# A one-layer decoder trunk on one core: new issue orders in the opening and in the experts' loop, and one more expert half in plain fp32

## The chip, the cores and the metric

The kernel runs on one core of one Trainium2 chip. The metric is the device time of one execution in microseconds (us). The time before is the median of three runs; a fourth execution was profiled, and every row of the trace is from that one.

## The reference

One layer with 512 rows of 1024 channels, batch 1, everything in fp32:

- `mod = silu(c) @ w_mod + b_mod` gives three vectors for each of the two halves (shift, scale, gate).
- `h = rms_norm(x) * (1 + sc1) + sh1`; `proj = h @ w_in` feeds three branches (a gated MLP over chunks, gated linear attention, sparse attention with a top-k of keys); `x = x + gt1 * (merged @ w_out)`.
- `h2 = rms_norm(x) * (1 + sc2) + sh2`, then a hierarchical mixture of experts: each row picks one of 4 groups, and in it 2 of 4 experts. For an expert with weights gate, up (1024 x 256 each) and down (256 x 1024):

```python
hg = h2 @ w_exp_gate[e]
hu = h2 @ w_exp_up[e]
y += (silu(hg) * hu * combine[:, e]) @ w_exp_down[e]
```

- `x = x + gt2 * y`.

## The kernel before

**Two kinds of product.** A product of fp32 matrices is mostly made of three products in a reduced type (fp32r). Each operand is split into a high and a low part by `split` (lines 226 and 227): ACT rounds the high part (`...h`), DVE subtracts it from the operand to get the low part (`...l`). `mm3` (line 217) then issues three matmuls, high by high, low by high and high by low. The other kind is the plain fp32 matmul (line 1574 for an expert's gate and up), which needs no split and reads the loaded weights as they are; the trace has two records for one such product of 512 columns.

**The opening** (0 to 59 us) computes the first six column tiles of `h @ w_in`. Its work is cut into some 400 steps, and the string `START` (lines 41 to 57) lists them in the order in which they are issued; a loop reads it and calls a small function for each. The steps that matter here: `wmN` issues N matmuls on a constant tile whose result nobody reads (line 396), so that TensorE is busy; `xeN` copies a finished bank of transposed rows to `xnT`, on ACT (line 319) or, with a V, on DVE (line 321); `whN` and `wlN` split a tile of `w_in` (lines 274, 277); `mp`, `ma`, `mb`, `mj`, `md`, `mo` and `mc` make, for one chunk of 128 channels, the shift and the scale from the loads of `w_mod` (products on ACT, line 331; sums and join on DVE, lines 338 and 342; columns on PE, lines 350 and 358; the final column on DVE, lines 366 and 367); `hh`, `hf` and `hl` make the transposed `h` of that chunk, high, full and low (lines 370, 374, 377); `fIDQ` is one matmul of column tile I with chunk D, Q being the pair of parts (line 387).

**The middle** (59 to about 582 us) holds the three branches and the router. The change does not touch it.

**The experts' loop** (lines 1780 to 1835) makes 17 passes. Passes 0 to 3 are the four experts of the first group, which share one tile of up to 128 rows. Passes 4 to 12 are single experts whose rows are fetched from DRAM by an indirect DMA on POOL (`slots`, line 1491); the pass `EX` = 6 is for rows that overflow the 128 of some expert: it takes its weights by a number known at run time, and pass 7 uses the same weights. Passes from `GL` = 13 are the last group, again on shared rows. Each pass e works on three things: gate and up of expert e (`gate_up`, line 1568, with the eight chunks of 128 channels in four calls of two, then `activate`, line 1578), the transposed activations and the down product of expert e-1 (`act_t`, line 1588; `down`, line 1607), and the weights and rows of expert e+1 (the units of `w_units`, line 1425, which split the weights into `guh`/`gul` and `dnh`/`dnl`; `x_rows`, line 1545, which transposes the rows `X` and splits them into `XTh`/`XTl`, or copies them to `XTf` for a plain half). `native` (line 1418) tells which halves of an expert's gate and up are plain. `overflow` (line 1721) is a generator of small DVE instructions that plan the overflow pass; the loop takes its steps one at a time (`next(ov)`).

**The loads.** 96 loads of 512 KB bring the experts' weights into 24 buffers (`load_raw`, line 1155). The load j+24 is issued when buffer j was last read: by the unit that splits it, or by `used` (line 1461) for a plain half. SP issues them, each behind a hold (line 1177) that reads the tile of an earlier load, so that SP goes on only once that one has landed; before the change this is the load with the number five less.

Of the kernel before, what the change touches and what calls it, by code (L numbers as in the profile page):

```python
# [13 lines left out]
I32 = mybir.dt.int32  # L14
# [22 lines left out]
HOLD_FROM, HOLD_TO, AHEAD = 26, 96, 5  # L37
# [1 line left out]
LV = [1, 2, 4, 8, 16, 32, 64]  # L39

START = """
Lx0 Lx1 Lx2 Lx3 wm9 Lm0 Lu0 Lm1 Lu1 Lm2 Lu2 sq0 sq1 rs0 sc0 sq2 rs1 xt0 sq3 rs2 sc1 sc2 wm3 xt1 rs3 xt2 mp0 sc3 ma0
wm3 xt3 mb0 xs7 xe0A xe2A md0 wh0 mo0 mp1 wl0V Lu3 Lm3 xe1A ma1 xe5A xe3A mc0 wh1 wm6 md1 mb1 hh0 wl1V Lu4 mo1 mp2
f000 md2 mc1 hf0 ma2 f001 hh1 f100 hl0V f101 hf1 mb2 f010 f002 f102 wh3 f011 mj2 f110 f111 hl1V mo2 xe4A f300 wl3V wh2
f302 f012 f112 f310 f312 mc2 mp3 f200 wl2V Lu5 Lm4 Lm5 Lm6 f202 f301 hh2 f210 f212 f311 ma3 hf2 f201 f211 f020 wh4 mb3
Lm7 f021 f120 f121 f220 xe6A f221 f320 f321 xe7A f400 mj3 f402 f410 hl2V mo3 wh5 f412 wl4V f022 f122 f222 f500 mp4 mc3
f502 f401 wl5V f411 hh3 f510 f512 f322 f420 hf3 ma4 f421 f501 f511 f422 mp5 hl3V f520 f521 f522 mb4 f030 f031 f032
f130 f131 f132 f230 mj4 f231 mp6 f232 ma5 mo4 f330 f331 mc4 f332 mb5 f430 hh4 f431 f432 f530 f531 hf4 f532 f040 f041
mp7 mj5 f140 f141 ma6 mo5 f240 mc5 f241 f340 mb6 f341 hh5 f440 f441 f540 f541 hf5 f050 f051 f150 mj6 f151 f250 hl5V
mo6 f251 hl4V f052 f152 mc6 f252 f042 ma7 f142 hh6 f242 f342 f442 mb7 hf6 f542 f350 f351 f352 f450 f451 f452 hl6V f550  # L50
# [122 lines left out]
def trunk(ctx: ExitStack, tc: tile.TileContext, I, out, dbg=None):  # L173
# [7 lines left out]
    V, A, G, T, SY = nc.vector, nc.scalar, nc.gpsimd, nc.tensor, nc.sync  # L181
# [953 lines left out]

    RAWS = ["E"] + ["X"] * 5 + ["MG", "MG", "T1", "T2"]
    NRAW = 2 * len(RAWS) + 4
    raws, ids, duo = {}, {}, {}
    wset = lambda e: e if e <= EX else e - 1

    EX, GL = 6, 13
# [12 lines left out]
    def load_raw(j, hold=False, eng=SY):  # L1154
        if j >= 96:
            return
        e, i = SEQ[j]
        if e >= PRE:
            if e not in ids:
                v = R.ex_i if e == EX else R.perm[:, e - PRE:e - PRE + 1]  # L1160
                ids[e] = nc.sync.value_load(v[0:1], min_val=0, max_val=15)
            e = ids[e]
        if j >= NRAW:
            raws[j] = raws[j - NRAW]
            if j % 2 == 0:
                duo[j] = duo[j - NRAW]
        elif j % 2:
            raws[j] = raws[j - 1, 1]
        else:
            k = RAWS[j // 2] if j < 2 * len(RAWS) else "P"  # L1170
            t = {"X": lambda: R.rawx.tile([128, 2048], FT, name="raw_x"),
                 "P": lambda: R.ep.tile([128, 2048], FT, name="raw_p", bufs=2)}.get(k, lambda: big(k, "raw_e"))()
            raws[j], raws[j, 1] = t[:, 0:1024], t[:, 1024:2048]
            duo[j] = t
        hf = i // 2 if i < 4 else i - 4
        if eng is SY and HOLD_FROM <= j < HOLD_TO:
            SY.value_load(raws[j - AHEAD][0:1, 0:1].bitcast(I32))
        eng.dma_start(raws[j], expert_src(e, i % 2 if i < 4 else 2)[:, hf * 1024:hf * 1024 + 1024])

    def load_x():  # L1180
# [235 lines left out]
    wfull = {}  # L1416

    def native(w):
        return (0, 1) if w < 2 else () if w in (3, EX) or w >= 12 else (1,)

    def native_dn(w):
        return (0, 1) if w == 0 else ()
# [47 lines left out]
    GR0 = range(4)  # L1470
# [46 lines left out]
    def x_group():  # L1517
        X = ep.tile([128, 1024], FT, name="X", bufs=1)
        A.activation(X[:, 0:512], st["X0"][0], AF.Copy)
        V.tensor_copy(X[:, 512:1024], st["X0"][1])  # L1520
        XT_[0], bs = [], []
        for hf in range(2):
            b = bank()
            for k in range(4):
                T.transpose(b[:, k * 128:(k + 1) * 128], X[:, 4 * hf + k::8], ident)
            bs.append(b)
        route()
        for hf in range(2):
            XT = ep.tile([128, 4, 128], FT, name="XTf", bufs=2)
            for k in range(4):  # L1530
                c, g, sh = bs[hf][:, k * 128:(k + 1) * 128], R.mcolx[:, 0, 4 * hf + k:4 * hf + k + 1], R.mcolx[:, 1, 4 * hf + k:4 * hf + k + 1]
                if hf:
                    V.tensor_scalar(XT[:, k], c, g, sh, OP.mult, OP.add)
                else:
                    A.activation(XT[:, k], c, AF.Identity, bias=sh, scale=g)
            XT_[0].append([XT])
        XT_[1] = XT_[0]

    def x_halves(hf):
        XT = [ep.tile([128, 4, 128], FR, name="XT" + x, bufs=2) for x in "hl"]  # L1540
        split(XT[0], XT[1], XT_[0][hf][0])
        for e in GR0[2 + hf:]:
            XT_[e] = [XT, XT_[0][1]] if hf == 0 else [XT_[2][0], XT]

    def x_rows(e):
        if e in GR0:
            return
        if e > GL:
            XT_[e] = XT_[GL]
            return  # L1550
        X = X_.pop(e)
        XT_[e] = []
        for hf in range(2):
            nat = hf in native(wset(e))
            XT = [ep.tile([128, 4, 128], FT, name="XTf", bufs=2)] if nat else [ep.tile([128, 4, 128], FR, name="XT" + x, bufs=2) for x in "hl"]
            b = bank()
            for k in range(4):
                T.transpose(b[:, k * 128:(k + 1) * 128], X[:, 4 * hf + k::8], ident)
            b = b.rearrange("p (k t) -> p k t", k=4)
            if nat:  # L1560
                A.activation(XT[0], b, AF.Copy)
            else:
                split(XT[0], XT[1], b)
            XT_[e].append(XT)
# [3 lines left out]
    def gate_up(e, kts):  # L1568
        if e not in gb:
            gb[e] = bank("mm")  # L1570
        for kt in kts:
            x, w = XT_[e][kt // 4], wfull[wset(e)][0][kt // 2]
            if len(w) == 1:
                T.matmul(gb[e], x[0][:, kt % 4], w[0][:, kt % 2], start=kt == 0, stop=kt == 7)
            else:
                mm3(gb[e], [t[:, kt % 4] for t in x], [t[:, kt % 2] for t in w], kt == 0, kt == 7)
# [200 lines left out]
    ov = overflow()  # L1777
    DN = []
    none = [lambda: None] * 10
    for e in range(NE - 1):  # L1780
        U = none[:4] + U[4:] if e == EX else w_units(wset(e + 1))
        gate_up(e, (0, 1))
        if e in (1, 2):
            x_halves(e - 1)
        for u in U[4:6] if e == EX else U[0:2]:
            u()
        for _ in range((0, 3, 1)[min(e, 2)]):
            next(ov, None)
        gate_up(e, (2, 3))
        used(e, 0)  # L1790
        if e == 0:
            ranks(range(4))
            positions()
            weights()
            one_hot(0)
            hi_lo(R.tw0.rearrange("p t e i -> p e t i"), R.PC[:, 0:4, 5:9])
        else:
            act_t(e - 1)
        for u in U[6:8] if e == EX else U[2:4]:
            u()  # L1800
        x_rows(e + 1)
        if e + 3 <= GL and e > 1:
            slots(e + 3)
        if e + 4 <= GL and e:
            one_hot(e + 4)
# [5 lines left out]
            down(e - 1)  # L1811
        for d in DN[:1]:
            d()
        gate_up(e, (6, 7))
        if e == 0:
            slots(0)
# [12 lines left out]
        for d in DN[1:]:  # L1829
            d()  # L1830
        used(e, 1)
        if e < NE - 2 and e not in (EX - 1, EX):
            U[6]()
            U[7]()
# [90 lines left out]
```

## Time and profile before

| | us |
|---|---|
| median of three runs | 784.78 |
| the three runs | 784.78, 779.66, 784.89 |
| the profiled execution, its own time | 781.99 |
| its span in the trace | 780.3 |
| busy in the span: PE | 744.3 (95%) |
| busy: DVE | 549.1 (70%) |
| busy: ACT | 327.6 (42%) |
| mean granted TensorE clock | 0.989 of full speed |

A timeline row reads: start, time from its start to the end of the last of its xcount instructions, engine, line, operation, output<-inputs, and in brackets how long the engine idled before it and what released it. PE is matmul, DVE VectorE, ACT ScalarE, POOL GpSimd, SPq the queue of SyncE. Matmuls are pipelined, so what one costs is the distance from its start to the next one's, not its duration. In a table by windows the columns are the window, its length, busy time and (count) for PE, weight loads, DVE, ACT and POOL, then the granted clock as a share of full speed, the DMA share and GB/s.

### The profile page before, as it was taken

The numbers are of one execution on the slowest core, as the hardware profiler recorded it, in microseconds if no ns is written. First come the engines' busy times: TensorE is split into PE (matmuls) and PEld (weight loads), VectorE is DVE, ScalarE is ACT, GpSimd is POOL, SyncE is SP. The second block draws the span as 40 slices with busy tenths as digits, with TensorE's granted clock in tenths as the row PEclk, the third lists the DMA queues.
The fourth block names the chain that finished last, engine by engine and source line by source line (L and its number), as shares of the span: only waits on it lengthen the run. The fifth ranks groups of instructions, "written<-read, shape, count | busy, mean of one in ns | idle before, by whom it ended". The sixth has DMA issues, their size and how long they took to land. (4 is left out here: it accounts for less than half of the span.)

```text
span 780.3 us, 11740 instructions
## 1 busy us (share of the span) xinstructions
PE 744.3 (95%) x4251; PEld 623.7 (80%) x4251; DVE 549.1 (70%) x1077; ACT 327.6 (42%) x583; POOL 125.2 (16%) x127
## 2 busy tenths in 40 slices
PE   7999999999999999999999999999999799899984
PEld 5888989998888899997788887889965577777763
DVE  5885557787579657756778677755567977887982
ACT  6765444414342333232444134434123644455760
POOL 1011002332110223300011122100000121321110
PEclk9999999999999999999999999999999999999998
DMA  8952253311221221476433766696465899999931
GB/s 351 341 190 79 82 176 109 108 55 61 76 81 55 82 81 55 160 221 202 158 124 113 244 209 220 181 303 260 143 234 180 318 349 355 329 328 360 319 106 29
DMA packets 53525, 144.88 MB, mean 186 GB/s; under 512 B 8349, under 2 KB 19762, under 8 KB 53210
## 3 DMA queue, kind: packets, MB, share of 16 engines
q1 hardware_dynamic: 44898, 130.00, 48.1%
q0 software_dynamic: 3024, 11.01, 5.7%
q10 hardware_dynamic: 5544, 3.10, 1.7%
q8 instruction: 34, 0.56, 0.3%
q14 instruction: 25, 0.20, 0.1%
HBM read 134.12 MB, written 11.29 MB: 186 GB/s over the span
## 5 line engine op out<-in xcount | busy, mean ns | idle before, releaser
L227 DVE TENSOR_TENSOR wlo<-raw,whi 128x1024 fp32r<-128x1024 f32 x70 | 88.7, 1271 | 59.9 <-ACT whi L226 59.8
L217 PE MATMUL bank_mm<-whi,hTh 128*128 128x256 f32 x352 | 101.0, 287 | 0.0
L217 PE MATMUL bank_mm<-whi,hTl 128*128 128x256 f32 x352 | 98.9, 281 | 0.0
L217 PE MATMUL bank_mm<-wlo,hTh 128*128 128x256 f32 x352 | 98.8, 281 | 0.0
L226 ACT ACTIVATE whi<-raw 128x1024 fp32r<-128x1024 f32 x70 | 73.1, 1054 | 48.9 <-DMA raw<-in_w_t_dram 29.9
L217 PE MATMUL bank_mm<-hTh,whi 128*128 128x512 f32 x224 | 92.5, 413 | 0.0
L217 PE MATMUL bank_mm<-hTh,wlo 128*128 128x512 f32 x224 | 88.8, 397 | 0.0
L217 PE MATMUL bank_mm<-hTl,whi 128*128 128x512 f32 x224 | 88.5, 395 | 0.0
L217 PEld LDWEIGHTS bank_mm<-whi,hTh 128*128 128x128 f32 x352 | 66.5, 189 | 0.6 <-issue 0.3
L217 PEld LDWEIGHTS bank_mm<-wlo,hTh 128*128 128x128 f32 x352 | 66.5, 189 | 0.2
L217 PEld LDWEIGHTS bank_mm<-whi,hTl 128*128 128x128 f32 x352 | 66.3, 188 | 0.0
L217 PE MATMUL bank_mm<-whi,mgs 128*128 128x256 f32 x256 | 50.2, 289 | 1.5 <-ACT mgs L229 1.0
L217 PEld LDWEIGHTS bank_mm<-hTh,whi 128*128 128x128 f32 x224 | 42.2, 188 | 11.0 <-issue 1.0
L217 PEld LDWEIGHTS bank_mm<-hTh,wlo 128*128 128x128 f32 x224 | 42.1, 188 | 10.3 <-DVE wlo L227 0.2
L217 PEld LDWEIGHTS bank_mm<-hTl,whi 128*128 128x128 f32 x224 | 42.2, 188 | 10.0 <-issue 0.7
L217 PE MATMUL bank_ms<-dnh,aT 128*128 128x512 f32 x120 | 43.5, 422 | 2.6 <-DVE aT L227 2.6
L978 DVE SCALAR_TENSOR_TENSOR acc<-raw,c_act,acc 128x1024 f32<-128x1024 f32 x28 | 38.0, 1368 | 7.8 <-DMA raw<-in_w_mod_dram 7.8
L217 PEld LDWEIGHTS bank_mm<-whi,mgs 128*128 128x128 f32 x256 | 41.0, 191 | 2.3 <-ACT mgs L229 1.4
L217 PE MATMUL bank_mm<-guh,XTh 128*128 128x512 f32 x88 | 38.9, 442 | 0.1
L217 PE MATMUL bank_mm<-gul,XTh 128*128 128x512 f32 x88 | 34.8, 396 | 1.8 <-DVE gul L227 1.8
L217 PE MATMUL bank_mm<-wlo,mgs 128*128 128x256 f32 x128 | 36.2, 283 | 0.0
L217 PE MATMUL bank_mm<-guh,XTl 128*128 128x512 f32 x88 | 34.9, 397 | 0.0
(450 smaller groups left out, 1697.1 us busy)
## 6 DMA issues: line engine op xcount, KB each, us to landing
raw<-in_w_t_dram SPq DMA_DIRECT2D x35, 512.0 KB, 3.3
raw<-in_w_mod_dram SPq DMA_DIRECT2D x32, 512.0 KB, 4.7
raw<-in_w_m_dram SPq DMA_DIRECT2D x24, 512.0 KB, 3.2
raw_e<-in_w_ed_dram SPq DMA_DIRECT2D x22, 512.0 KB, 7.3
wmod<-in_w_ms_dram SPq DMA_DIRECT2D x16, 512.0 KB, 9.4
raw_x<-in_w_eg_dram SPq DMA_DIRECT2D x16, 512.0 KB, 10.0
raw_x<-in_w_eu_dram SPq DMA_DIRECT2D x16, 512.0 KB, 9.6
raw<-in_w_branch_dram SPq DMA_DIRECT2D x12, 512.0 KB, 3.4
```

The source lines that it names most:

```text
L217: T.matmul(o, l[a], r[b], start=first and i == 0, stop=last and i == 2)
L226: A.activation(hi, src, AF.Copy)
L227: (eng or V).tensor_tensor(lo, src, hi.bitcast(FT), OP.subtract)
L978: V.scalar_tensor_tensor(acc[:, c], raw, c_act[:, kt:kt + 1], acc[:, c], OP.mult, OP.add)
```

## The change

The diff, cut to its core. Of the table `START` only one line of each is shown; the instructions that it moves stand below.

```diff
-Lx0 Lx1 Lx2 Lx3 wm9 Lm0 Lu0 Lm1 Lu1 Lm2 Lu2 sq0 sq1 rs0 sc0 sq2 rs1 xt0 sq3 rs2 sc1 sc2 wm3 xt1 rs3 xt2 mp0 sc3 ma0
+Lx0 Lx1 Lx2 Lx3 wm20 Lm0 Lu0 Lm1 Lu1 Lm2 Lu2 sq0 sq1 rs0 sc0 sq2 rs1 xt0 sq3 rs2 sc1 sc2 wm3 xt1 rs3 xt2 mp0 sc3 ma0
...
-    raws, ids, duo = {}, {}, {}
+    raws, ids, duo, sent = {}, {}, {}, []
...
         if eng is SY and HOLD_FROM <= j < HOLD_TO:
-            SY.value_load(raws[j - AHEAD][0:1, 0:1].bitcast(I32))
+            SY.value_load(raws[sent[-AHEAD]][0:1, 0:1].bitcast(I32))
+        sent.append(j)
...
     def native(w):
-        return (0, 1) if w < 2 else () if w in (3, EX) or w >= 12 else (1,)
+        return (0, 1) if w < 3 else () if w in (3, EX) or w >= 12 else (1,)
...
-        XT_[1] = XT_[0]
+        XT_[1] = XT_[2] = XT_[0]
...
-        for e in GR0[2 + hf:]:
-            XT_[e] = [XT, XT_[0][1]] if hf == 0 else [XT_[2][0], XT]
+        XT_[3] = [XT, XT_[0][1]] if hf == 0 else [XT_[3][0], XT]
 
-    def x_rows(e):
+    def x_rows(e, hfs=(0, 1)):
...
         gate_up(e, (0, 1))
-        if e in (1, 2):
-            x_halves(e - 1)
+        if e == 2:
+            x_halves(0)
+            x_halves(1)
         for u in U[4:6] if e == EX else U[0:2]:
             u()
-        for _ in range((0, 3, 1)[min(e, 2)]):
-            next(ov, None)
-        gate_up(e, (2, 3))
-        used(e, 0)
+        gate_up(e, (2,))
         if e == 0:
             ranks(range(4))
...
         else:
             act_t(e - 1)
+        for _ in range(2 if e == 1 else 0):
+            next(ov)
+        gate_up(e, (3,))
+        used(e, 0)
         for u in U[6:8] if e == EX else U[2:4]:
             u()
-        x_rows(e + 1)
-        if e + 3 <= GL and e > 1:
+        x_rows(e + 1, (0,) if e == EX else (0, 1))
+        if e + 3 <= GL and e > 1 and e != EX:
             slots(e + 3)
...
             down(e - 1)
         for d in DN[:1]:
             d()
+        if e:
+            next(ov, None)
         gate_up(e, (6, 7))
...
         used(e, 1)
+        if e == EX:
+            x_rows(e + 1, (1,))
+            slots(e + 3)
```

So: the third expert's first half is plain like its second; the two splits of the shared rows are made in pass 2, for the fourth expert alone; the transposes of the activations stand one product earlier in each pass; the overflow steps stand elsewhere; in pass 6 the second half of the next pass's rows and the fetch for pass 9 stand at the end; a hold looks at the fifth load issued before it instead of the load numbered five less. In the rest of `START` the second filler `wm6` becomes `wm8`, a third (`wm5`) stands between the first matmuls, `xe3` goes to DVE and stands earlier, `hh0` and `hf0` stand before the second weight split, and the column of chunk 1 stands later.

DVE in the opening, from the first low part of a weight tile (`wlo`) to the join of chunk 2 (line 342; `mc` is a final column, `macc` a running sum). Before:

```order
L277 TENSOR_TENSOR wlo<-raw,whi 128x1024
L338 SCALAR_TENSOR_TENSOR macc<-wmod,c_act,mpg 128x256 x2
L366 TENSOR_SCALAR mc<-bank_ms,bsc,pv 128x1
L367 TENSOR_SCALAR mc<-bank_ms,pv 128x1
L338 SCALAR_TENSOR_TENSOR macc<-wmod,c_act,macc 128x256 x2
L277 TENSOR_TENSOR wlo<-raw,whi 128x1024
L366 TENSOR_SCALAR mc<-bank_ms,bsc,pv 128x1
L367 TENSOR_SCALAR mc<-bank_ms,pv 128x1
L338 SCALAR_TENSOR_TENSOR macc<-wmod,c_act,mpg 128x256 x2
L377 TENSOR_TENSOR hTl<-hf,hTh 128x512
L338 SCALAR_TENSOR_TENSOR macc<-wmod,c_act,macc 128x256 x2
L342 TENSOR_TENSOR macc<-macc 128x256
```

Now, one row longer; the join of chunk 2 (line 342) is the row behind the last one shown:

```order
L321 COPY xnT_121<-bank_ms 128x512
L277 TENSOR_TENSOR wlo<-raw,whi 128x1024
L366 TENSOR_SCALAR mc<-bank_ms,bsc,pv 128x1
L367 TENSOR_SCALAR mc<-bank_ms,pv 128x1
L338 SCALAR_TENSOR_TENSOR macc<-wmod,c_act,mpg 128x256 x2
L338 SCALAR_TENSOR_TENSOR macc<-wmod,c_act,macc 128x256 x2
L377 TENSOR_TENSOR hTl<-hf,hTh 128x512
L366 TENSOR_SCALAR mc<-bank_ms,bsc,pv 128x1
L367 TENSOR_SCALAR mc<-bank_ms,pv 128x1
L277 TENSOR_TENSOR wlo<-raw,whi 128x1024
L338 SCALAR_TENSOR_TENSOR macc<-wmod,c_act,mpg 128x256 x2
L338 SCALAR_TENSOR_TENSOR macc<-wmod,c_act,macc 128x256 x2
```

One copy of `xnT` has come in at the head, the low part of chunk 0's `h` (line 377) stands ahead of the second `wlo`, and the column of chunk 0 (lines 366, 367) ahead of the sums of the next chunk.

DVE in passes 1 and 2 (`perm` is the last instruction of the overflow steps there, `act` an activation, `dnl` and `gul` low parts of weights, `oh`, `wsl` and `idx` belong to `slots`). Before:

```order
L1743 CAST perm<-PP 128x5
L227 TENSOR_TENSOR gul<-raw_x,guh 128x2x256 x2
L1478 TENSOR_TENSOR oh<-cst,PP 128x512
L227 TENSOR_TENSOR dnl_6009<-raw_e,dnh_6008 128x1024
L1585 SCALAR_TENSOR_TENSOR act<-act,w_5874,bank_mm 128x256
L1499 COPY wsl<-bank_ms 128x2
L1500 TENSOR_TENSOR wsl<-wsl 128x1
L1488 CAST idx<-bank_ms 128x1
L227 TENSOR_TENSOR dnl_6030<-raw_e,dnh_6029 128x1024
L227 TENSOR_TENSOR XTl<-XTf,XTh 128x512
L227 TENSOR_TENSOR gul<-raw_e,guh 128x2x256 x2
```

Now:

```order
L1743 CAST perm<-PP 128x5
L1585 SCALAR_TENSOR_TENSOR act<-act,w_5893,bank_mm 128x256
L1500 COPY wsl<-bank_ms 128x2
L1501 TENSOR_TENSOR wsl<-wsl 128x1
L1489 CAST idx<-bank_ms 128x1
L227 TENSOR_TENSOR dnl_6018<-raw_e,dnh_6017 128x1024
L227 TENSOR_TENSOR XTl<-XTf,XTh 128x512 x2
L227 TENSOR_TENSOR gul<-raw_e,guh 128x2x256 x2
```

The low parts of the third expert's first half are gone, here and in one more row of two ahead of the overflow steps; `oh` and the first `dnl` now stand among those steps, and the two splits of the shared rows together.

ACT in passes 5 and 6 (`XTh` are the high parts of the rows for pass 7 at the row that changes, `dnh` of down weights). Before:

```order
L226 ACTIVATE guh<-raw_e 128x2x256 x2
L226 ACTIVATE aT<-bank_ms 128x256
L226 ACTIVATE guh<-raw_e 128x2x256 x2
L226 ACTIVATE XTh<-bank_ms 128x512 x2
L226 ACTIVATE dnh_6639<-raw_e 128x1024
L1580 ACTIVATE act<-bank_mm 128x256
L226 ACTIVATE dnh_6652<-raw_e 128x1024
L226 ACTIVATE guh<-raw_e 128x2x256 x2
```

Now:

```order
L226 ACTIVATE guh<-raw_e 128x2x256 x2
L226 ACTIVATE aT<-bank_ms 128x256
L226 ACTIVATE guh<-raw_e 128x2x256 x2
L226 ACTIVATE XTh<-bank_ms 128x512
L226 ACTIVATE dnh_6614<-raw_e 128x1024
L1580 ACTIVATE act<-bank_mm 128x256
L226 ACTIVATE dnh_6631<-raw_e 128x1024
L226 ACTIVATE XTh<-bank_ms 128x512
L226 ACTIVATE guh<-raw_e 128x2x256 x2
```

The second `XTh` has moved behind the activation and both `dnh`.

## Rows read from the trace of the kernel before

**Rows 1.** Table by windows, core 0, five stretches of the span.
```profile
20.18:59.04 38.86, 38.86 (x178) 32.01 (x178) 32.88 (x71) 25.80 (x39) 3.32 (x3) 0.96 0.73 263
59.04:582.00 522.96, 514.28 (x3243) 453.49 (x3241) 355.43 (x655) 190.18 (x347) 86.70 (x92) 1.00 0.44 142
...
604.54:634.54 30.00, 24.65 (x112) 18.34 (x112) 26.49 (x67) 16.90 (x31) 3.32 (x3) 1.00 0.89 310
634.54:661.66 27.12, 27.12 (x120) 20.28 (x121) 20.11 (x41) 12.04 (x22) 5.88 (x4) 1.00 1.03 370
661.66:671.47 9.81, 7.54 (x33) 6.33 (x32) 9.13 (x19) 6.17 (x11) 3.29 (x2) 0.83 0.98 347
```
**Rows 2.** Timeline of PE in the opening.
```profile
1.25 4.02 PE L396 MATMUL bank_ms<-wmm 128*128 128x512 bf16 x9 [1.25 <-DVE wmm L281]
7.62 0.33 PE L314 MATMUL bank_ms<-ident,xa 128*128 128x128 f32 x1 [2.34 <-DVE xa L308]
...
24.50 0.85 PE L358 MATMUL bank_ms<-ones_c,macc 128*128 128x1 f32 x4
25.21 0.69 PE L387 MATMUL bank_ms<-hTh,whi 128*128 128x512 f32 x1
...
31.34 0.50 PE L358 MATMUL bank_ms<-ones_c,macc 128*128 128x1 f32 x4
```
**Rows 3.** Table by windows of one microsecond, at the slow clock.
```profile
24.00:25.00 1.00, 1.00 (x5) 0.83 (x4) 1.00 (x2) 1.00 (x2) 0.00 (x0) 0.50 0.78 311
```
**Rows 4.** Timeline of DVE in the opening.
```profile
15.40 1.22 DVE L277 TENSOR_TENSOR wlo<-raw,whi 128x1024 fp32r<-128x1024 f32 x1 [1.53 <-ACT whi L274]
...
22.98 0.42 DVE L342 TENSOR_TENSOR macc<-macc 128x256 f32<-128x256 f32 x1
```
**Rows 5.** Timeline of PE in passes 1 to 4.
```profile
593.56 3.68 PE L1574 MATMUL bank_mm<-raw_x,XTf 128*128 128x512 f32 x8
...
605.32 0.39 PE L217 MATMUL bank_mm<-guh,XTh 128*128 128x512 f32 x1
605.55 0.39 PE L217 MATMUL bank_mm<-gul,XTh 128*128 128x512 f32 x1
...
607.61 0.50 PE L217 MATMUL bank_mm<-gul,XTh 128*128 128x512 f32 x1 [1.21 <-DVE gul L227]
...
609.74 0.51 PE L1591 MATMUL bank_ms<-ident,act 128*128 128x128 f32 x2 [0.70 <-DVE act L1585]
...
613.67 0.73 PE L217 MATMUL bank_ms<-dnh,aT 128*128 128x512 f32 x2 [0.79 <-DVE aT L227]
...
623.82 0.58 PE L1497 MATMUL bank_ms<-twx,oh 128*128 128x4 f32 x4 [1.97 <-ACT XTf L1561]
...
634.54 0.61 PE L1497 MATMUL bank_ms<-twx,oh 128*128 128x4 f32 x4 [0.68 <-DVE aT L227]
```
**Rows 6.** Timeline of DVE in pass 2.
```profile
606.27 1.29 DVE L227 TENSOR_TENSOR gul<-raw_x,guh 128x512 fp32r<-128x512 f32 x2
```
**Rows 7.** Timelines of ACT, DVE and PE in passes 5 and 6.
```profile
661.64 0.60 ACT L226 ACTIVATE XTh<-bank_ms 128x512 fp32r<-128x512 f32 x1 [4.69 <-PE bank_mm L217]
...
666.26 0.41 DVE L1582 TENSOR_TENSOR act<-act,bank_mm 128x256 f32<-128x256 f32 x1
...
666.82 0.48 PE L1591 MATMUL bank_ms<-ident,act 128*128 128x128 f32 x2 [2.27 <-DVE act L1582]
```
**Rows 8.** DMA issues, size where it is known, median us from issue to landing.
```profile
modb<-h_d,idx POOLq DMA_INDIRECT x5, 8.2
```
**Rows 9.** Timelines of DVE and PE in one of the last passes.
```profile
732.85 0.42 DVE L227 TENSOR_TENSOR aT<-bank_ms,aT 128x256 fp32r<-128x256 f32 x1
...
733.32 0.73 PE L217 MATMUL bank_ms<-dnh,aT 128*128 128x512 f32 x2 [0.57 <-DVE aT L227]
```
**Rows 10.** Timelines of SP's queue and of ACT at one of the last loads.
```profile
737.05 2.21 SPq L1178 DMA_DIRECT2D raw_p<-in_w_ed_dram  x2
...
741.90 1.14 ACT L226 ACTIVATE guh<-raw_e 128x512 fp32r<-128x512 f32 x2
```

More of the change, by code (lines that the diff above doesn't have):

```diff
@@ L41 @@
 START = """
-Lx0 Lx1 Lx2 Lx3 wm9 Lm0 Lu0 Lm1 Lu1 Lm2 Lu2 sq0 sq1 rs0 sc0 sq2 rs1 xt0 sq3 rs2 sc1 sc2 wm3 xt1 rs3 xt2 mp0 sc3 ma0
[L43 to L47, printed above, removed]
+Lx0 Lx1 Lx2 Lx3 wm20 Lm0 Lu0 Lm1 Lu1 Lm2 Lu2 sq0 sq1 rs0 sc0 sq2 rs1 xt0 sq3 rs2 sc1 sc2 wm3 xt1 rs3 xt2 mp0 sc3 ma0
+wm3 xt3 mb0 xs7 xe0A xe3V xe2A md0 wh0 mo0 mp1 wm8 wl0V Lu3 Lm3 mc0 xe1A ma1 xe5A hh0 md1 mb1 hf0 f000 f001 wh1 mo1
+hl0V mp2 f002 mc1 wl1V Lu4 f100 hh1 wm5 f101 md2 ma2 f102 hf1 mb2 f010 wh3 f011 mj2 f110 f111 hl1V mo2 xe4A f300 wl3V
+wh2 f302 f012 f112 f310 f312 mc2 mp3 f200 wl2V Lu5 Lm4 Lm5 Lm6 f202 f301 hh2 f210 f212 f311 ma3 hf2 f201 f211 f020 wh4
+mb3 Lm7 f021 f120 f121 f220 xe6A f221 f320 f321 xe7A f400 mj3 f402 f410 hl2V mo3 wh5 f412 wl4V f022 f122 f222 f500 mp4
+mc3 f502 f401 wl5V f411 hh3 f510 f512 f322 f420 hf3 ma4 f421 f501 f511 f422 mp5 hl3V f520 f521 f522 mb4 f030 f031 f032
 f130 f131 f132 f230 mj4 f231 mp6 f232 ma5 mo4 f330 f331 mc4 f332 mb5 f430 hh4 f431 f432 f530 f531 hf4 f532 f040 f041
@@ L1550, in x_rows @@
             return
-        X = X_.pop(e)
-        XT_[e] = []
-        for hf in range(2):
+        X = X_[e]
+        XT_.setdefault(e, [])
+        for hf in hfs:
             nat = hf in native(wset(e))
```

## The prediction

> **What bounds the kernel now.** I read the page first: PE is busy for 95% of the span, so a change can only win where PE stands still, runs at the lower clock, or does work that goes. The table by windows says where that is [rows 1]. From 59.04 to 582 us PE works 514.28 of 522.96 us, and no edit falls there; that stretch only starts earlier or later. Three stretches have something to give: the opening, where PE is never idle but the mean granted clock is 0.96; 604.54 to 634.54 us (passes 2 to 4 of the experts' loop), where PE works 24.65 of 30.00 us; and 661.66 to 671.47 us (pass 6), where it works 7.54 of 9.81 us at a mean clock of 0.83. Then I read the timelines of PE for each gap and its releaser, and those of the releaser for what stood ahead of it [rows 2 to 9]. The loads come last, since their share is 1.03 and 0.98 in two of the stretches [rows 1, 10].
>
> **The opening.** In one microsecond of it the granted clock is 0.50, the lower of the two levels, 1.2 GHz [rows 3]. There the four column matmuls of chunk 2 take 0.71 us from start to start (24.50 to 25.21) where the same four take 0.37 later (31.34 to 31.71), or 0.50 to their modelled end [rows 2]. The first matmul of column tile 3 begins behind them at 25.21, and from there PE has no gap. The columns wait for the join on DVE, which ends at 22.98 + 0.42 = 23.40 [rows 4]. The change puts a copy (0.6 us at most, as ACT's) on DVE ahead of the low part that had idled 1.53 us [rows 4], so the copy is covered; every other DVE row up to the join is the same set in another order. If PE keeps the full clock, the columns run from 23.40 to 23.90, and tile 3 begins 25.21 - 23.90 = 1.31 us earlier. The window's clock bounds that: (1 - 0.96) x 38.86 = 1.55 us is all that the clock can give there [rows 1].
>
> The fillers: 11 more at the start, two more in the second group, five new ones. Nine took 4.02 us, 0.45 each [rows 2], partly at the lower level; at the full one I estimate half, 0.22. The eleven fall into the gap of 2.34 us before the first transpose [rows 2], and 11 x 0.22 = 2.4 just fit. The other seven stand ahead of the first matmuls or among them, where PE waits for the parts of `h` and for the column of chunk 2; as the join at 23.40 sets the end, I take zero. Uncovered, seven cost 7 x 0.22 = 1.5. Bounds of the opening: 1.55 won to 1.5 lost; I take **-1.3**.
>
> **Passes 1 to 4.** Three gaps stand in a row: 1.21 us (a low part of the third expert's first half), 0.70 (its DVE queue, now at the activation) and 0.79 (the same, now at `aT`), together 2.70 us [rows 5]. DVE is full there, 26.49 of 30.00 us [rows 1]. The change takes four low parts off it, 2 x 1.29 = 2.58 us [rows 6], and four high parts off ACT, and it moves the last overflow steps and a down weight's split ahead of the activation. What was late by 2.70 in all is then early by about the same, so the three gaps go. What is late next: the gap of 1.97 behind the copy to `XTf` and that of 0.68 behind `aT` [rows 5]; both hang on the row transposes and on PE's own results, so they move along with PE, and I give them nothing.
>
> The price is on PE. Eight records of the plain product run from 593.56 to about 597.1, so one product costs two times 0.44 = 0.88 us; one fp32r product costs 605.55 - 605.32 = 0.23, three 0.69 [rows 5]. Four chunks go from three fp32r products to one plain one: 4 x (0.88 - 0.69) = +0.77. The Trainium skill has a rule that speaks against this edit ("FP8 and Floating Point Precision", TensorE Precision Notes): a true fp32 product takes four passes through the array. Four passes of 0.23 would be 0.92, and the edit +0.92 instead of +0.77; the row of 0.88 decides. Bounds: all of 2.70 with the plain product nearly free (-2.7) to no gap closed (+0.8). I take -2.70 + 0.77 = **-1.9**.
>
> **Pass 6.** PE waits 2.27 us for the activation on DVE (666.26), that one for the activation on ACT; ACT had idled 4.69 us on a PSUM bank for the second half of pass 7's rows (`XTh`, 661.64), and both `dnh` and the activation stood behind it [rows 7]. Behind this gap the clock falls: the stretch lost (1 - 0.83) x 9.81 = 1.67 us of work at the lower level [rows 1]. The change puts this `XTh` behind the activation and the two `dnh`; ACT then waits for the bank only after them. The activation comes when its own bank is full, and PE goes on with the second half's work of the pass. So 2.27 + 1.67 = 3.94 go. No other gap in the loop was followed by the lower level, so with the gap I let the fall go too. What is late next: the fetch for pass 9 now goes out at the end of pass 6. Its one-hot tile, small matmul and index stand behind the activation, which I expect near 663.2 us; 8.2 us later it has landed [rows 8], at 671.4. The pass that transposes these rows then comes to them near 672.3, so 0.9 is to spare, and I charge 0.15 for a fetch that is slower. Bounds: 3.94 won to nothing won. I take **-3.8**.
>
> **Edits at nothing.** The transposes of the activations stand one product (0.69 us) earlier in each pass. In the last passes PE waits about 0.6 us each time for `aT` on DVE (0.57 at 733.32), but there DVE made `aT` at 732.85 right behind low parts of gate and up, not behind the transposes [rows 9]; it stays where it is. Bounds: 0 to -1.8, three such gaps. The hold on the fifth load issued before costs nothing as long as that load has landed; the two refills of the third expert's first half go out later, behind four more loads.
>
> **Sum.** -1.3 - 1.9 - 3.8 = -7.0 on the profiled execution: 781.99 becomes 774.99. The four executions before (784.78, 779.66, 784.89, 781.99) have a mean of 782.83, and their median run is 1.95 above it; I put the changed kernel at that mean less 7.0, **775.8 us**. Its own range is 772.5 to 778.5: the opening 0.3 more or 0.6 less, passes 1 to 4 0.8 more or less, pass 6 1 less, the last passes up to 1.8 more, and a median of three that scatters by about 2.
>
> **Rivals.**
> - *The clock falls in the opening all the same* (0.15). For it: PE was busy for all of the slow microsecond [rows 3], so a busy PE alone did not keep the clock. Against it: the fillers close the gap of 2.34 us and put more columns among the first matmuls [rows 2]. The 1.3 goes: 775.8 + 1.3 = 777.1.
> - *Pass 6 finds another wait* (0.15). The `XTh` now stands ahead of the next gate and up split on ACT, and the fetch for pass 9 has under one microsecond to spare. If PE waits as long there, and the clock falls behind it, the 3.8 does not come: 779.6. Against it: ACT is busy for only 6.17 of 9.81 us there [rows 1].
> - *The loads become the bound* (0.10). From 634.54 to 661.66 us their share is 1.03 and they move 370 GB/s [rows 1]; at that rate 512 KB take 1.42 us, and two refills behind four more loads land up to 5.7 us later. One of the last loads had landed by 737.05, when the hold behind it let go, and its split began at 741.90 [rows 10], 4.85 us to spare. If the delay reaches it, and PE starts 7 us earlier, PE waits anything from 0.2 to 5.7: 776 to 781.5, middle 779. The Trainium skill ("DMA: Bandwidth & Descriptors", Specifications) gives about 358 GB/s as the limit of a core, by which the loads could come no faster than they do; the 370 over 27 us lie above it, so I give this rival no more than 0.10.
> - *The added PE work lands on the path and the gaps stay* (0.05): the slower side. Place: PE in the opening and in pass 2. Eleven fillers at 0.45 are 4.9, less the gap of 2.34 [rows 2] +2.6; seven more at 0.45 +3.1; the plain products +0.8; together +6.5, on the mean 782.83 + 6.5 = 789.3 if no gap closes. It decides if fewer than 6.5 us of the gaps go; with the lower clock behind the gaps that stay it could reach 1% over the median.
>
> **How the numbers follow.** The forecast has 0.55, the rivals 0.15, 0.15, 0.10 and 0.05. One per cent of 784.78 is 7.85, about what a measurement of this kernel can tell from no change; faster means under 776.9. Of the forecast's chance about 0.43 lies below that (its middle is 1.1 under it, its range reaches 1.6 over), of the first rival 0.08, of the second 0.02, of the third 0.03: faster 0.56. Slower means above 792.6, which the last rival reaches only with the lower clock on top: 0.03, and 0.41 is left for no change. The range from 771 to 782 takes in the forecast with the last passes' gain, and the first three rivals; it leaves out the slower side.
>
> **What would show it.** Right: the changed profile has a clock near 1.00 from 20 to 59 us with tile 3 beginning near 23.9; no gap of over 0.5 us on PE between the first product of expert 2 and its down product; no gap at `act` in pass 6 and a clock of 1.00 there. Wrong: the window of pass 6 is still near 10 us; new gaps of PE on `raw` loads after 700 us; a start of the middle later than 59.0.

## The result, and the profile after

| | before | after |
|---|---|---|
| median, six runs each (us) | 784.69 | 776.39 |
| lowest to highest | 779.66 to 787.44 | 772.08 to 778.93 |
| profiled execution, its own time | 781.99 | 776.66 |
| its span | 780.3 | 774.8 |
| mean granted clock of that execution | 0.989 | 0.994 |

The ratio is 0.9892, with a 95% interval from 0.9864 to 0.992: the changed kernel is faster by 1.1%. The forecast was 775.8. Ratios leave out slow executions; among all kernels here that is one, of 784.48 us, of the kernel *changed, old order*. The single runs of either kernel lie up to 8 us apart, so the profiles (5.3 us apart) and the medians (8.3 apart) need not agree.

By windows, the changed kernel's stretches beside those of [rows 1] (the columns are the same):

```profile
20.18:58.00 37.82, 37.73 (x178) 30.35 (x178) 32.98 (x69) 25.22 (x38) 1.64 (x3) 1.00 0.73 271
58.00:580.00 522.00, 512.93 (x3240) 453.07 (x3239) 354.07 (x648) 189.67 (x346) 86.64 (x92) 1.00 0.44 141
...
601.00:630.00 29.00, 27.21 (x103) 18.49 (x102) 23.75 (x66) 15.12 (x27) 3.29 (x3) 0.94 0.95 353
630.00:656.00 26.00, 25.20 (x111) 18.00 (x111) 22.47 (x45) 14.25 (x26) 5.86 (x4) 1.00 1.03 390
656.00:666.00 10.00, 10.00 (x56) 8.66 (x55) 9.21 (x20) 6.36 (x11) 2.87 (x2) 1.00 1.03 348
```

The opening and pass 6 (656 to 666) run at the full clock, and pass 6 has no idle PE left. But passes 2 to 4 now show 0.94 where they had 1.00 (the last section comes back to this).

The timeline of PE after, at the places of [rows 2, 5, 7]:

```profile
23.75 0.50 PE L358 MATMUL bank_ms<-ones_c,macc 128*128 128x1 f32 x4
24.34 0.49 PE L387 MATMUL bank_ms<-hTh,whi 128*128 128x512 f32 x1
...
582.57 1.13 PE L1526 MATMUL bank_ms<-ident,X 128*128 128x128 f32 x8 [0.88 <-DVE X L1521]
...
610.83 0.73 PE L217 MATMUL bank_ms<-dnh,aT 128*128 128x512 f32 x2 [0.18 <-DVE aT L227]
...
620.63 0.58 PE L1498 MATMUL bank_ms<-twx,oh 128*128 128x4 f32 x4 [1.61 <-DVE aT L227]
...
633.14 0.61 PE L1498 MATMUL bank_ms<-twx,oh 128*128 128x4 f32 x4 [0.59 <-DVE aT L227]
...
654.49 0.50 PE L217 MATMUL bank_mm<-gul,XTh 128*128 128x512 f32 x1 [0.18 <-DVE gul L227]
...
662.82 0.39 PE L1591 MATMUL bank_ms<-ident,act 128*128 128x128 f32 x2
...
728.40 0.73 PE L217 MATMUL bank_ms<-dnh,aT 128*128 128x512 f32 x2 [0.60 <-DVE aT L227]
```

Of the three gaps of passes 1 and 2 (1.21, 0.70, 0.79) one of 0.18 is left. The wait of 2.27 at the transposes of pass 6 is gone (662.82 has no bracket). The waits of passes 3 and 4 are there still, 1.61 and 0.59, and that of the last passes too, 0.60. On DVE the reason is plain; here is its timeline of the changed kernel ahead of `aT`:

```profile
617.66 2.49 DVE L227 TENSOR_TENSOR gul<-raw_p,guh 128x512 fp32r<-128x512 f32 x4
620.07 0.42 DVE L227 TENSOR_TENSOR aT<-bank_ms,aT 128x256 fp32r<-128x256 f32 x1
...
725.52 2.49 DVE L227 TENSOR_TENSOR gul<-raw_x,guh 128x512 fp32r<-128x512 f32 x4
727.93 0.41 DVE L227 TENSOR_TENSOR aT<-bank_ms,aT 128x256 fp32r<-128x256 f32 x1
```

`aT` stands behind four low parts of weights in pass 3 as in the last passes. That those are not wanted yet is shown by the kernel *aT first* below.

On ACT in pass 6, the second `XTh` (661.28) now stands behind the activation and both `dnh`; no wait of 4.69 us as in [rows 7]:

```profile
660.05 0.38 ACT L1580 ACTIVATE act<-bank_mm 128x256 f32<-128x256 f32 x1 [0.99 <-PE bank_mm L217]
660.33 1.05 ACT L226 ACTIVATE dnh<-raw_e 128x1024 fp32r<-128x1024 f32 x1
661.28 0.59 ACT L226 ACTIVATE XTh<-bank_ms 128x512 fp32r<-128x512 f32 x1
```

### The profile page after: what moved, and what is told of

The parts are those of the page before. It is cut to its first block, busy times and chain, and to the rows that moved or that the text cites. A ratio compares the mean times of both kernels' runs of the same rounds, so it can differ in the third digit from the quotient of the medians.

```text
span 774.8 us, 11755 instructions
## 1 busy us (share of the span) xinstructions
PE 746.0 (96%) x4265; PEld 621.6 (80%) x4265; DVE 547.1 (71%) x1074; ACT 325.0 (42%) x578; POOL 120.4 (16%) x127
## 5 line engine op out<-in xcount | busy, mean ns | idle before, releaser
L226 ACT ACTIVATE dnh<-raw_e 128x1024 fp32r<-128x1024 f32 x22 | 23.2, 1055 | 31.6 <-PE bank_ms L217 31.6
L227 DVE TENSOR_TENSOR dnl<-raw_e,dnh 128x1024 fp32r<-128x1024 f32 x22 | 26.9, 1221 | 10.6 <-ACT dnh L226 10.2
```

Of the source, the lines that this page charges most:

```text
L226: A.activation(hi, src, AF.Copy)
L227: (eng or V).tensor_tensor(lo, src, hi.bitcast(FT), OP.subtract)
```

## The experiments

Four groups of kernels ran, each group beside runs of the kernel before on its chip (medians of before: 783.6, 783.5, 787.0 and 782.6), so ratios are compared. Because single runs scatter by several microseconds, each profile was also read in pieces: where the opening's last matmul starts, where the loop starts (the row transposes that stand at 582.66 in before), and how long the loop takes from there to the start of PE's last matmul. For before the two rows are

```profile
582.66 1.13 PE L1525 MATMUL bank_ms<-ident,X 128*128 128x128 f32 x8 [0.87 <-DVE X L1520]
...
768.30 0.39 PE L217 MATMUL bank_ms<-guh,aT 128*128 128x512 f32 x1
```

and the loop takes 768.30 - 582.66 = 185.6 us. All kernels, read in the same way:

| kernel | ratio to before (95%) | clock, 0 to 59 us | loop starts | loop takes | clock, 604 to 634 us |
|---|---|---|---|---|---|
| before | 1 | 0.94 | 582.7 | 185.6 | 1.00 |
| changed | 0.9892 (0.9864 to 0.9920) | 1.00 | 582.6 | 180.8 | 0.94 |
| changed, again | 0.9883 (0.9840 to 0.9926) | 0.97 | 585.6 | 179.3 | 1.00 |
| changed, old opening | 0.9900 (0.9868 to 0.9932) | 0.91 | 584.5 | 179.2 | 1.00 |
| before, new opening | 0.9982 (0.9953 to 1.0010) | 1.00 | 580.6 | 187.1 | 0.94 |
| before, plain half | 0.9957 (0.9938 to 0.9977) | 0.97 | 582.4 | 183.1 | 1.00 |
| changed, half split | 0.9972 (0.9945 to 0.9999) | 1.00 | 583.5 | 184.5 | 0.89 |
| before, new pass 6 | 0.9969 (0.9939 to 0.9999) | 1.00 | 579.1 | 183.6 | 0.94 |
| changed, old pass 6 | 0.9967 (0.9944 to 0.9991) | 0.97 | 582.2 | 185.3 | 0.94 |
| changed, old order | 0.9922 (0.9899 to 0.9945) | 1.00 | 581.2 | 179.6 | 1.00 |
| changed, aT first | 0.9823 (0.9799 to 0.9847) | 0.91 | 586.1 | 175.4 | 1.00 |
| changed, 4th half plain | 0.9870 (0.9836 to 0.9904) | 1.00 | 581.4 | 178.6 | 1.00 |
| both of these | 0.9828 (0.9787 to 0.9870) | 1.00 | 580.3 | 175.1 | 1.00 |
| aT first, old opening | 0.9866 (0.9824 to 0.9908) | 0.88 | 585.2 | 176.2 | 1.00 |

Each row's last four columns are from one profile. At the same clock the changed loop came out within 0.1 us in two of them (179.3 and 179.2, with either opening), but the loop of *aT first* came out 0.9 apart (175.4 and 176.2), where a fetch landed later. Where the clock of 604 to 634 us is 0.94 the same loop is 1.5 longer (180.8 for 179.3, 187.1 for 185.6). So a difference of some tenths in one profile's loop is not shown by that number alone.

**The opening, put back and alone.** The edit swaps the whole string `START` for the other kernel's:

```diff
-Lx0 Lx1 Lx2 Lx3 wm20 Lm0 Lu0 Lm1 Lu1 ...
+Lx0 Lx1 Lx2 Lx3 wm9 Lm0 Lu0 Lm1 Lu1 ...
```

> The changed kernel with the opening order of before put back; all else as changed. Theory of the forecast: the opening gave 1.3 us (0.9 us at the start of the middle in the changed kernel's trace), so this kernel stands at 776.4 + 0.9 to 1.3 = 777.3 to 777.7 us and its first matmul of column tile 3 begins near 25.2 us with the clock at 0.50 before it. Rival: the middle waits for loads that do not start earlier and gives the opening's gain back, as the changed kernel's trace shows (0.89 us ahead at 60 us, 0.09 at 582 us): then 776.4 within 0.5.

> The kernel before with the new opening order alone. Theory of the forecast: 784.7 - 0.9 to 1.3 = 783.4 to 783.8 us. Rival (given back in the middle): 784.7 within 0.5, with PE ahead of before by 0.9 us at 60 us and by under 0.3 at 582 us.

Measured 776.81 us (0.9900) and 782.81 us (0.9982). Neither differs from its partner beyond the intervals. Nor do the pieces settle it. Over the five profiles with the old opening the opening's last matmul starts at 59.81 us on average (single ones from 57.00 to 61.84) and the loop at 582.76; over the nine with the new one at 58.55 (57.60 to 62.49) and 582.61. These ranges lie over each other, so a shorter opening is not shown.

What the new order does bring is a higher clock. The mean granted clock of whole executions, over all timed runs, is higher with it in all three comparisons: 0.993 for 0.989 (changed kernel), 0.989 for 0.986 (kernel before) and 0.994 for 0.988 (the kernel *aT first* below). But the order has a price that the forecast put at nothing, and one profile shows it: in *before, new pass 6* the old opening happened to run at 1.00 throughout. Its column of chunk 2, its first matmul of column tile 3 and the last of the opening:

```profile
23.14 0.58 PE L358 MATMUL bank_ms<-ones_c,macc 128*128 128x1 f32 x4
23.58 0.48 PE L387 MATMUL bank_ms<-hTh,whi 128*128 128x512 f32 x1
...
57.00 0.39 PE L387 MATMUL bank_ms<-hTl,mg 128*128 128x512 f32 x1
```

The changed kernel, also at 1.00, has that column at 23.75 and that matmul at 24.34. Before them PE works through the five new fillers, 21.36 - 20.14 = 1.22 us:

```profile
20.14 1.25 PE L396 MATMUL bank_ms<-wmm 128*128 128x512 bf16 x5
21.36 0.50 PE L387 MATMUL bank_mm<-hTh,wlo 128*128 128x512 f32 x1
...
57.78 0.40 PE L387 MATMUL bank_ms<-hTl,mg 128*128 128x512 f32 x1
```

All six profiles of the new order at 1.00 end between 57.60 and 58.18. So at the full clock the new opening is 0.6 to 1.2 us longer than that one profile of the old, while profiles in which the clock fell end between 58.80 and 61.84 with the old order and between 58.83 and 62.49 with the new.

In the profiled pair the changed kernel is 1.02 us ahead at the end of the opening (57.78 for 58.80) and 0.09 at the start of the loop. Part of that goes at a wait for a transfer from DRAM at 362 us, on DVE and then on PE. Before:

```profile
362.28 0.29 DVE L1086 SCALAR_TENSOR_TENSOR L<-bank_ms,bt 128x128 f32<-128x128 f32 x1 [1.73 <-DMA bt<-m_d]
...
364.25 0.33 PE L1097 MATMUL bank_ms<-ident,L 128*128 128x128 f32 x1 [0.47 <-DVE L L1093]
```

After:

```profile
362.40 0.29 DVE L1086 SCALAR_TENSOR_TENSOR L<-bank_ms,bt 128x128 f32<-128x128 f32 x1 [1.89 <-DMA bt<-m_d]
...
364.38 0.33 PE L1097 MATMUL bank_ms<-ident,L 128*128 128x128 f32 x1 [1.02 <-DVE L L1093]
```

The transfer's data come at the same time in both, and the kernel that is ahead waits longer (1.02 instead of 0.47). But the middle does not always take a lead back. In the kernel before with the new opening alone the opening ends 1.18 us earlier than in before and the loop starts 2.03 earlier (580.63), and over all 14 profiles a late opening goes with a late loop: 57.00 with 579.07, 61.84 with 585.22, 62.49 with 586.08. The middle itself takes from 522.1 to 526.8 us, which hides one microsecond either way.

**The plain half, alone and put back.** Alone it needs the new hold too: with a plain half the loads no longer leave in the order of their numbers, and the load numbered five less has not been issued at some holds. So the pacing is part of this edit and was not tried apart.

```diff
-        return (0, 1) if w < 2 else () if w in (3, EX) or w >= 12 else (1,)
+        return (0, 1) if w < 3 else () if w in (3, EX) or w >= 12 else (1,)
```

> The kernel before with the third expert's first half plain, and the hold by issue order that this needs; opening, pass 6 and the order of the loop as before. Forecast's term: the three gaps of passes 1 and 2 go (2.70 us) for 0.8 us of plain products, 784.0 - 1.9 = 782.1 us. Second theory, from the kernel with the half split again (5.4 us slower than the changed one): the half is worth about 5 us wherever it stands, 779 us. Third: without the moved overflow steps DVE stays late, and gaps of 1 us or more remain between the first product of the third expert and its down product: 783 to 784.

> The changed kernel with the third expert's first half split again (12 fp32r products instead of 4 plain ones, its high and low parts on ACT and DVE, the first row split back in pass 1). Theory: most of the three gaps of passes 1 and 2 (2.70 us) return and the plain products' 0.8 us go: 776.4 + 1.9 = 778.3 us. Rival: the moved overflow steps had freed DVE already and the plain half only cost PE time: 776.4 - 0.8 = 775.6 us.

Alone: 779.61 us, near the second theory's 779; by the ratio of 0.9957 it is 3.4 us, and the loop is 185.6 - 183.1 = 2.5 us shorter, between the first theory and the second. Its PE timeline from the first product of the third expert:

```profile
604.24 3.68 PE L1574 MATMUL bank_mm<-raw_x,XTf 128*128 128x512 f32 x8
607.76 0.39 PE L1591 MATMUL bank_ms<-ident,act 128*128 128x128 f32 x2
...
610.97 0.73 PE L217 MATMUL bank_ms<-dnh,aT 128*128 128x512 f32 x2 [0.19 <-DVE aT L227]
```

The gaps go without any moved step (0.19 is left at 610.97), so the third theory falls. The four plain products take 607.76 - 604.24 = 3.52, 0.88 each, as reckoned.

Put back: 781.77 us (0.9972), 0.8% slower than the changed kernel where 0.2% was expected. With the half split, the new order is worse than the old one; its PE and DVE timelines:

```profile
607.38 0.50 PE L217 MATMUL bank_mm<-gul,XTh 128*128 128x512 f32 x1 [0.47 <-DVE gul L227]
...
610.56 0.70 PE L1592 MATMUL bank_ms<-ident,act 128*128 128x128 f32 x2 [2.44 <-DVE act L1586]
...
607.24 0.69 DVE L1479 TENSOR_TENSOR oh<-cst,PP 128x512 fp32r<-128x512 f32 x1
607.84 1.22 DVE L227 TENSOR_TENSOR dnl<-raw_e,dnh 128x1024 fp32r<-128x1024 f32 x1
608.98 0.17 DVE L1685 CAST twx<-eb 128x4 fp32r<-128x4 f32 x1
...
610.03 0.47 DVE L1586 SCALAR_TENSOR_TENSOR act<-act,w,bank_mm 128x256 f32<-128x256 f32 x1
```

The overflow steps from 608.98 now stand ahead of the activation; with low parts on DVE too, PE waits 2.44 us there, and from 608 to 616 us the clock is 0.62. So the moved steps need the time that the plain half frees.

**Pass 6, alone and put back.**

```diff
-        x_rows(e + 1)
-        if e + 3 <= GL and e > 1:
+        x_rows(e + 1, (0,) if e == EX else (0, 1))
+        if e + 3 <= GL and e > 1 and e != EX:
...
+        if e == EX:
+            x_rows(e + 1, (1,))
+            slots(e + 3)
```

> The kernel before with the order of pass 6 alone changed. Forecast's term: the wait of 2.27 us and the lower clock behind it (1.7 us) go, 3.8 us less: 784 - 3.8 = 780.2 us, a ratio of 0.995. Second theory, from the changed kernel with the old pass 6, which is 0.8% slower than the changed one: the edit is worth 6 us wherever it stands, 0.992. Third: with the loop later than in the changed kernel the fetch for pass 9 or the bank is late, and less than 2 us go, over 0.9975.

> The changed kernel with the order of pass 6 of before put back (both halves of pass 7's rows and the fetch for pass 9 ahead of the activation). Theory: the wait of 2.27 us at the activations of pass 6 and the lower clock behind it return: 776.4 + 3.4 to 3.9 = 779.8 to 780.3 us, PE idle near 2.3 us ahead of the transposes of pass 6. Rival: the wait is set by DVE's and ACT's load in passes 5 and 6 and not by the place of the second split; then it stays away and the time is 776.4 within 0.5. A second rival: the wait returns but the clock does not fall: 778.7.

Alone: 780.18 us (0.9969), put back: 780.75 us (0.9967). In the kernel with the old order put back the wait returns, and larger than in before:

```profile
665.51 0.67 PE L1591 MATMUL bank_ms<-ident,act 128*128 128x128 f32 x2 [3.48 <-DVE act L1582]
```

Its loop takes 185.3 us against the 180.8 of the changed kernel at the same clock in passes 2 to 4, so the edit is worth 4.5 there; the rival that the place does not matter falls. So does the one by which the clock would not fall: from 656 to 680 us it is 0.93. Alone the edit is worth 3.5 in the loop (183.6 for the 187.1 of *before, new opening*, which is before's loop at the same clock of 0.94). That is less, because the wait it removes is 2.27 there and not 3.48, and because a new wait stands in its place. In the kernel with the edit alone the rows of the fetch that was moved to the end of the pass come late:

```profile
672.78 1.16 PE L1558 MATMUL bank_ms<-ident,modb 128*128 128x128 f32 x8 [0.67 <-DMA modb<-h_d,idx]
```

**The order of transposes and overflow steps.**

```diff
-        gate_up(e, (2,))
+        for _ in range((0, 3, 1)[min(e, 2)]):
+            next(ov, None)
+        gate_up(e, (2, 3))
+        used(e, 0)
...
-        for _ in range(2 if e == 1 else 0):
-            next(ov)
-        gate_up(e, (3,))
-        used(e, 0)
...
-        if e:
-            next(ov, None)
```

> The changed kernel with the transposes of the activations and the overflow steps back at their places of before (the plain half, pass 6 and the opening as changed). Theory: DVE is short of time in passes 1 and 2 only by what the plain half freed, and the order is worth no more than the 0.18 us gap left there: 776.4 within 0.6. Rival: the moved steps are part of the gain; gaps of 0.5 to 1.5 us come back at the activation of pass 1 or at aT, and the lower clock may follow: 777.5 to 779.5.

776.83 us (0.9922), the median of the eleven executions that the ratio takes; with the twelfth it is 777.45. By the intervals the time is not told apart from the changed kernel's, and no gap came back at the activation of pass 1. The loop takes 179.6 us against 179.3, with the wait of pass 3 at 1.97 instead of 1.61 and that of pass 4 at 0.68 instead of 0.59, so some 0.4 us may be due to the new order; one profile does not show it.

**Taking `aT` out of the queue.** If `aT` is late because DVE makes four low parts first, moving two of them behind it must show it.

```diff
-        for u in U[4:6] if e == EX else U[0:2]:
-            u()
+        late = e > 1 and e != EX
+        if not late:
+            for u in U[4:6] if e == EX else U[0:2]:
+                u()
         gate_up(e, (2,))
...
             act_t(e - 1)
+        if late:
+            for u in U[0:2]:
+                u()
```

> The changed kernel with the first two units of the next expert's gate and up behind the transposes of the activations instead of ahead of them, from pass 2 on. Theory: in the changed kernel PE still waits for aT 1.61 us in pass 3, 0.59 in pass 4 and three times 0.6 in the last passes because DVE makes aT behind four low parts; with two of them behind it aT comes 1.2 us earlier, so 1.2 + 0.6 + 1.8 = 3.6 us go and the lower clock behind the 1.61 with them in the runs that had it: 771 to 772.8 us. Rival: DVE then stands idle for the transposes and the low parts are late at the next products instead, 776.4 or more.

769.07 us (0.9823): faster than both kernels, clear of the changed kernel's interval. By the ratio, on the 784.7 that the theory starts from, it is 770.8, at the lower end of the theory's 771 to 772.8. The loop takes 175.4 us, 3.9 less than the changed one at the full clock. DVE and PE of this kernel:

```profile
620.71 1.28 DVE L227 TENSOR_TENSOR gul<-raw_p,guh 128x512 fp32r<-128x512 f32 x2
621.91 0.42 DVE L227 TENSOR_TENSOR aT<-bank_ms,aT 128x256 fp32r<-128x256 f32 x1
...
622.48 0.58 PE L1498 MATMUL bank_ms<-twx,oh 128*128 128x4 f32 x4 [0.41 <-DVE aT L227]
...
653.89 0.50 PE L217 MATMUL bank_mm<-gul,XTh 128*128 128x512 f32 x1 [0.19 <-DVE gul L227]
...
673.72 1.16 PE L1558 MATMUL bank_ms<-ident,modb 128*128 128x128 f32 x8 [0.59 <-DMA modb<-h_d,idx]
```

The wait of 1.61 is 0.41, that of pass 4 and the three at `aT` in the last passes are gone, and the low parts behind `aT` are late nowhere that they were not before: the two waits for a `gul` that are left (0.19 at 653.89, 0.61 at 753.31) stand in the changed kernel too. The fetch of pass 6 is now 0.59 us late, as it was (0.67) in the kernel with the new pass 6 alone.

**The fourth expert's second half plain, and both edits.**

```diff
-        return (0, 1) if w < 3 else () if w in (3, EX) or w >= 12 else (1,)
+        return (0, 1) if w < 3 else () if w == EX or w >= 12 else (1,)
...
-            x_halves(1)
```

> The changed kernel with the fourth expert's second half plain too (12 fp32r products become 4 plain ones, one row split and four weight splits go). Theory: aT of pass 3 stands behind two low parts instead of four, so the wait of 1.61 us falls by 1.2 us for 0.8 us of plain products, and the lower clock behind it (1.7 us in the profiled run) stays away: 776.4 - 0.4 to - 2.1 = 774.3 to 776.0 us. Rival: two more refills go out later and loads become late: over 777, with waits for raw tiles on ACT in the last passes.

> Both edits that beat the changed kernel together: the next expert's first units behind the transposes of the activations, and the fourth expert's second half plain. Theory: both shorten the same wait of pass 3 (0.41 and 0.40 us left of 1.61), so the second edit adds only its price on PE less what is left of that wait: 769.1 + 0.8 - 0.4 = 769.5 us within 1. Rival: the DVE time that the plain half frees is worth more, as it was for the third expert, and the two add up: 765 to 767 us.

Alone 772.12 us (0.9870; on 784.7 that is 774.5, inside the theory's range), its loop 0.7 shorter than the changed one at the full clock; both together 771.38 us (0.9828). The two do not add up: the loop of both (175.1) is 0.2 shorter than with the first alone, and the ratios are the same. PE waited for no load of weights in either, so the two later refills cost nothing.

**Once more, and the opening under the better loop.** The changed kernel itself was run again, and the better loop with the old opening.

> The changed kernel once more, so that it and the two kernels below are timed beside the same runs of the kernel before. Both theories: the ratio of its first measurement, 0.9892 within its interval, some 775 to 777 us, with a mean granted clock near 0.993 against 0.986 of the kernel before.

> The kernel with the units behind the transposes, with the opening order of the kernel before. Theory (the opening's gain is given back in the middle): the same time as with the new opening within 0.7, 768.4 to 769.8 us, though its clock is lower by 0.003 to 0.004. Rival (the gain counts once the waits of the loop are gone): 0.9 to 1.3 us slower, 770 to 770.4.

776.77 us (0.9883), and 775.01 us (0.9866). The latter is slower than either theory had it (768.4 to 770.4) and slower than its partner (0.9823), but the two were timed beside different groups of the kernel before, and the intervals overlap. Its loop is 0.9 longer, the fetch of pass 6 coming 1.46 us late; its opening ran at 0.88. Whether the opening is worth something in the median stays open: three comparisons give 0.1% to 0.4% for it, none clear of its interval.

## Why the prediction was right

The side is right and the time is 0.6 off (776.4 for 775.8). The two larger terms came by their mechanism; the third, the opening, is not shown. Part of the closeness is luck: the 7.0 was taken off the mean of four executions, 782.83. Taken off the median of six, 784.69, it gives 777.7, and the medians fell by 8.3.

- **Opening, -1.3.** The clock held at 1.00, and the join ended at 22.92 + 0.42 = 23.34 on DVE in the changed profile (23.40 reckoned). Two steps failed. Column tile 3 began at 24.34, not 23.9: zero was taken for the fillers among the first matmuls, but five of them took 1.22 us of PE, which was still at work until 23.75, and the tile's first part waited for its load on ACT:

```profile
23.23 1.06 ACT L274 ACTIVATE whi<-raw 128x1024 fp32r<-128x1024 f32 x1 [1.44 <-DMA raw<-in_w_t_dram]
```

  And "that stretch only starts earlier or later" does not describe 59 to 582 us: it varies by 4.7 us of itself, and in the profiled pair a wait for a transfer took back part of the lead, so that the loop began no earlier (582.57 for 582.66). What the opening is worth at the end of the run stays open.
- **Passes 1 to 4, -1.9.** The three gaps went as said, by the plain half alone, and the waits of passes 3 and 4 stayed. The reason given for those two, that they hang on the row transposes and on PE's own results, was wrong in part: with two low parts moved behind `aT` the one is 0.41 and the other gone. The loop won 2.5. (The price is 4 x 0.19 = 0.76, not 0.77, which changes nothing.) The term that was too small is the price of a gap: idle time was counted, but PE also loses around it. The timeline of PE in before around the first of the three gaps, of which [rows 5] has the middle row:

```profile
606.01 0.39 PE L217 MATMUL bank_mm<-guh,XTh 128*128 128x512 f32 x1
...
607.95 0.39 PE L217 MATMUL bank_mm<-guh,XTl 128*128 128x512 f32 x1
```

  From 606.01 to the product at 607.61 are 1.60 us where 0.23 is usual, and to the next 0.34: 1.37 + 0.11 = 1.48 lost, where the row says 1.21. I had also left out that a wait that stays may let the clock fall. With the lower level behind the wait of 1.61 the loop of the changed kernel took 1.5 us more in its first profile than in its second, which had the same wait at the full clock.
- **Pass 6, -3.8.** 3.5 in the loop alone, 4.5 against the changed kernel with the old order. The part for the clock is shown as well: in all four profiles with the wait (2.27 or 3.48 us) the mean clock of 656 to 680 us is 0.93, in the ten without it 1.00. Two readings on the way were wrong. In before:

```profile
654.84 1.06 PE L1558 MATMUL bank_ms<-ident,modb 128*128 128x128 f32 x8
...
661.21 0.39 PE L217 MATMUL bank_mm<-gul,XTh 128*128 128x512 f32 x1
...
662.27 0.69 DVE L227 TENSOR_TENSOR XTl<-bank_ms,XTh 128x512 fp32r<-128x512 f32 x1 [3.78 <-ACT XTh L226]
...
663.08 0.37 ACT L1580 ACTIVATE act<-bank_mm 128x256 f32<-128x256 f32 x1
```

  The `XTh` of 661.64 did not wait for a PSUM bank: the transposes into its bank were done by 655.90. The tile `XTh` has two buffers, and the one it takes over was read until 661.60 by PE's last product of pass 6 with an `XTh`. (From 661.66 us on PE is at the products of pass 7; what is called the window of pass 6 is where its activations are transposed.) And ACT's part of the activation was done by 663.45, long before DVE's at 666.26: DVE's own queue was late, because the `XTl` of the same rows had stood there for 3.78 us behind that `XTh`. The edit moves both out of the way, so the term comes out all the same. The fetch that was charged 0.15 was on time in both profiles of the changed kernel and in three more with this order, and late by 0.43 to 1.46 in five others: "under one microsecond to spare" was right.
- **Edits at nothing.** The earlier transposes gave nothing in the last passes, for the reason given; the kernel that moves `aT` itself shows it. For the order of the steps 0.4 at most was seen, in one profile.
- **The sum by parts.** Alone, opening, plain half and pass 6 give 0.18, 0.43 and 0.31%, together 0.92 of the 1.1%; put back, plain half and pass 6 cost 0.8% each. The parts lean on each other, so taking one out of the finished kernel overstates it.
- **Rivals.** That the clock falls in the opening anyway was seen with the new order too, in three of nine profiles (0.91, 0.97, 0.97), with the old in four of five. The loads did not become the bound of the loop, though 390 GB/s were moved from 630 to 656 us: PE waited for no load of weights. The limit of about 358 GB/s for a core in the Trainium skill ("DMA: Bandwidth & Descriptors", Specifications), a stack's rate halved between two cores, lies below that rate of a kernel on one core; these rows do not bear it out. The plain products cost what was reckoned and the gaps they were to pay for went; the five fillers that stand on PE's path cost 0.24 each, near the 0.22 reckoned, but were counted at nothing.

## What to carry to other kernels

When an engine waits for a small result, look at what stands ahead of that result in the producer's own queue; work that is not wanted yet belongs behind it, and here this was worth 0.7%, more than any single part of the change alone. Before you count a gain at the start of a program, ask how much the stretch behind it scatters, and whether it waits for transfers whose start does not move; here 4.7 us of scatter hid a term of 1.3. Count filler work at its full price wherever the engine is otherwise busy. Where runs scatter by more than the effect, compare a shorter stretch (the loop), and say apart which clock it had and which transfers came late, since both move it.

## What was not expected

- The same wait is followed by the lower clock in one execution and not in another. By windows of the two profiles of the changed kernel, with the wait of 1.61 us in both, the first execution and then the second:

```profile
604.00:634.00 30.00, 27.60 (x114) 19.65 (x114) 24.99 (x60) 18.28 (x33) 3.29 (x3) 0.94 0.97 379
```

```profile
604.00:634.00 30.00, 28.17 (x117) 19.14 (x116) 26.36 (x70) 17.46 (x32) 3.29 (x3) 1.00 0.99 374
```

  The change is not the cause: of nine profiles with a wait of 1.61 or 1.97 us at this place three show the lower clock behind it, among them *before, new opening*, which has the loop of before. In *before, new pass 6* the clock fell behind the first of the three gaps instead (0.74 from 604 to 609 us). So a wait of PE has two prices, and what a shorter wait gains in the median depends on how often the dearer one falls due. The mean clock over all timed runs was 0.986 for before (29 runs of the first group) and 0.993 for the changed kernel (six runs); 0.007 of 780 us are 5.5, an estimate of how much of the gain came through the clock at most.
- The start of the loop lies between 579.1 and 586.1 us in 14 profiles of programs that differ little up to there: these 7 us are about as much as the runs of one kernel scatter.
